# Another written order for the first block of a two-block model: which matmul stands behind which

## The chip, the cores and the metric

The kernel runs on one core of a Trainium2 chip. A core has a matmul engine (TensorE; in the profile PE, and PEld for its weight loads), VectorE (DVE), ScalarE (ACT) and GpSimd (POOL), which run beside each other and wait for each other through semaphores; SyncE (SP) issues most DMAs. The metric is the device time of one execution in microseconds (us), lower is better. The kernel before takes 1187.47 us, the median of three runs (1187.04 to 1188.63).

## The reference, cut to what matters

One sequence of 256 tokens with 1024 features goes through two blocks. Only the first is touched. It projects the normed input `h` with one wide matrix into the inputs of three branches and into the logits of three gates, and adds the gated branches:

```python
h = rms_norm(x, norm1_g[l])
proj = h @ w_in[l]
p_rwkv, p_sb, q_mem, gate_logits = jnp.split(proj, cut, axis=-1)
y_a, v_first = rwkv7_branch(p_rwkv, ...)         # recurrence over time, 8 heads
y_b = stick_breaking_branch(p_sb, ...)           # causal attention, 8 heads
y_m = memory_branch(q_mem, mem, ...)             # softmax attention on 256 memory rows, 4 heads
ys = jnp.stack([y_a, y_b, y_m], axis=2)
branch_out = jnp.einsum('btnc,ncd->btnd', ys, w_branch[l])
gates = jax.nn.sigmoid(gate_logits.reshape(b, t, N_BRANCH, D_MODEL))
x = x + jnp.sum(gates * branch_out, axis=2) @ w_out[l]
x = x + conv_ffn(x, ...)
```

The memory branch makes its keys and values from the normed memory: `kv = rms_norm(mem, mem_g) @ w_kv`, keys in the first 512 columns, values in the other 512. The second block (an mLSTM mixer, a sparse attention and two more FFNs) follows.

## The kernel before, in words

**Weights.** Every weight matrix is cut into tiles of 128 x 128, and `weight_tiles` (L59) lays them in DRAM in the order in which the program uses them, eight to a block of 512 KB. `Stream` (L220) loads a block over SP's queue into one of three buffers (`wstg`), and splits it into a rounded high part on ScalarE (`whi`, L238) and the rest on VectorE (`wlo`, L239), three buffers each. `W.take` hands out the next tiles and sees to it that blocks up to two ahead are asked for. A product with a tile is three matmuls: high by high, high by low part of the activations, low by high. `fp_tile` (L368) makes 128 output features for all 256 tokens from 8 (or 4) tiles; `tp_group` (L381) makes 512 output columns with tokens on the partitions, from 32 tiles, four at a time.

**The written order.** The first block is traced under a manual schedule for TensorE: its instructions run as the program writes them, up to `order.close()` (L1062). The other engines' order, and that of SP's DMAs, is set by a planner that simulates the program. To interleave the small matmuls of the branches with the weight products, each branch is a Python generator, a chain. `flow.tick` (L277) is called for each weight tile; at every tile whose number is a multiple of `GRID`, each chain whose time has come runs up to its next `yield n`, which asks to be called again n tiles later. A step writes its matmuls into TensorE's order at once, behind the tiles so far; `flow.join` (L285) writes all that is left of a chain in one go.

**The order before**, by number of weight tiles taken. 0 to 64: keys of the memory (32 tiles, accumulators from `ps_r`), then its values; beside them `x1_chain` (L523) makes the normed input X1, and the keys are normed and transposed (`qk_feat`, L509). 64 to 176: `rw_proj` (L886), 14 x 8 tiles for the RWKV branch, its chain `run_rwkv` (L701) beside it. 176 to 304: four `tp_group`s, queries of the memory, then queries, keys and values of the attention (L986 to L991); each is normed on ScalarE and VectorE, and transposed on TensorE 16 tiles after its chain has started. 304 to 592: three rounds of eight, one round for each branch (L999): a gate of 8 tiles into the left half of a PSUM accumulator, `Tanh` of it on ScalarE, a branch product of 4 tiles into the right half of the same accumulator, and the gated sum on VectorE. There are four such accumulators (`ps_acc`). The memory is the first round, the attention the second, the RWKV the third; before a round's first product its chain is joined.

**The RWKV chain** computes norms of the keys (`rw_norms`), prepares and scores four pairs of heads (`rw_prep`, `rw_scores`), then inverts small triangular blocks: the blocks `rw_ba` go to DRAM and come back in another layout (L742, L743), VectorE solves them in 15 steps (L746, L748), the results go to DRAM again (L751) and come back into `rw_krv` and `rw_z` by 24 small loads (L753, L756), all issued by SP. `yield 64` (L757) stands between this and the first matmul on the results (`rw_lt`, L774). Two levels of products and four steps of a scan follow, and the output norm. **The attention chain** `sticks` (L941) has per pair of heads: scores (`sb_z`), mask and softplus on VectorE and ScalarE, a cumulative sum on TensorE (`sb_c`), exponential, and the product with the values (`sb_o`). Its work buffer `sb_ze` shares one buffer (tag `sbt`) with `rw_ba`.

Of the kernel before, what the change touches and what calls it, by code (L numbers as in the profile page):

```python
# [18 lines left out]
KD = D // 128  # L19
# [7 lines left out]
STARTS = (82, 148, 181, 247, 279)  # L27
GRID = 2
HEAD = 4
# [13 lines left out]
def _tp(w):  # L43
    k, n = w.shape
    return w.reshape(k // 128, 128, n // 512, 4, 128).transpose(2, 0, 3, 1, 4).reshape(-1, 128, 128)
# [13 lines left out]
def weight_tiles(i):  # L59
    w_in = i["w_in"][0]  # L60
    rw = _fp(w_in[:, :1792]).reshape(14, KD, 128, 128)[RWKV_ORDER].reshape(-1, 128, 128)
    out = [_tp(i["w_mem_kv"][0]), rw, _tp(w_in[:, 3328:3840]), _tp(w_in[:, 1792:3328])]
    for n in (2, 1, 0):
        g = _fp(w_in[:, 3840 + n * D:3840 + (n + 1) * D]).reshape(KD, KD, 128, 128)
        b = _fp(i["w_branch"][0, n]).reshape(KD, 4, 128, 128)
        out.append(np.concatenate([g, b], axis=1).reshape(-1, 128, 128))
    out += [_fp(i["w_out"][0]), _up(i["w_up"][0], True), _fp(i["w_down"][0])]
    aw = i["a_w_in_2"][0]
    gt = np.zeros((D, 128), np.float32)
    gt[:, 0:4] = aw[:, 3072:3076]  # L70
    gt[:, 32:36] = aw[:, 3076:3080]
    out += [_fp(gt), _fp(aw[:, :1024]), _tp(aw[:, 1024:2048]), _fp(aw[:, 2048:3072]),
            _fp2(i["a_w_out_2"][0]), _up(i["f_w_up_2"][0], False), _fp(i["f_w_down_2"][0])]
    wkv = i["w_kv_2"]
    for g in range(2):
        s = slice(g * 512, (g + 1) * 512)
        out += [_tp(i["b_w_q_2"][0][:, s]), _tp(wkv[:, :D][:, s])]
    out.append(_tp(wkv[:, D:]))
    out += [_fp2(i["b_w_o_2"][0]), _up(i["f_w_up_2"][1], False), _fp(i["f_w_down_2"][1])]
    return out  # L80
# [111 lines left out]
def body(tc, a, out, voff, coff, tap=None, upto=99):  # L192
# [11 lines left out]
    def ps_acc(name="acc"):  # L204
        return psum.tile([128, 512], F32, name=name, tag="acc", bufs=4)
# [14 lines left out]
    class Stream:  # L220
        pos = 0
        hi, lo = {}, {}
# [157 lines left out]

    def tp_group(X, ps=ps_acc):  # L381

        po = [ps(), ps()]
        for k in range(KD):
            hi, lo = W.take(4)
            for tt in range(2):
                s = slice(tt * 128, (tt + 1) * 128)
                PE.matmul(po[tt], X.H[:, k, s], hi, start=(k == 0), stop=False)  # L388
                PE.matmul(po[tt], X.L[:, k, s], hi, start=False, stop=False)  # L389
                PE.matmul(po[tt], X.H[:, k, s], lo, start=False, stop=(k == KD - 1))  # L390
            flow.tick(4)
        return po
# [111 lines left out]
    def s4(name):  # L504
        return mp.tile([128, 4, T], F32, name=name, tag=s4tag[name])
# [3 lines left out]
    def qk_feat(po, st, nh, gain, name):  # L509
        rs = head_rs(po, nh, st and st.ev, name)  # L510
        dst = feat[name] = s4(name)
        qn = [normed(po, tt, rs, nh, name + "n") for tt in range(2)]
        yield 16
        for tt in range(2):
            tok_to_feat(qn[tt], dst, tt, gain)

    def v_tok(X, st, dst):
        po = tp_group(X)
        for tt in range(2):
            A.activation(dst[:, tt], po[tt], AF.Identity, scale=st.rs[:, tt:tt + 1] if st else 1.0, bias=0.0)  # L520
        return dst

    def x1_chain():  # L523
        yield 20
        sm._rows()
        yield 20
        s1._rows()
        yield 10
        s1._spread()
        for k in range(KD):  # L530
            V.scalar_tensor_tensor(x0[:, k], x0[:, k], vec("norm1_g", k), s1.bc, op0=OP.mult, op1=OP.mult)
            split(X1.H[:, k], X1.L[:, k], x0[:, k])
# [18 lines left out]
    x1c = flow.start(x1_chain())  # L551
    pmk = tp_group(XM, ps_r)
    flow.start(qk_feat(pmk, sm, 4, vec("mem_k"), "mkT"))
    mv = s4("mv").rearrange("p a t -> p (a t)").rearrange("p (a c) -> p a c", c=512)
    v_tok(XM, sm, mv)
    flow.join(x1c)
# [68 lines left out]
    def rw_prep(p, rs, SC, BK, UV, wc):  # L625
# [33 lines left out]
        for par in range(2):  # L659
# [5 lines left out]
            V.tensor_tensor(BK[s, p, :, o], ch(kp, par), ch(iw, par), op=OP.mult)  # L665
        yield 14
        PE.matmul(pb[:, T:2 * T], con("bones"), sx, start=True, stop=True)
# [33 lines left out]
    def run_rwkv():  # L701
# [10 lines left out]
        while em.i < 6:  # L712
            yield 1
        yield 8
        rs = rw_norms()
        for p in range(4):
            while em.i < 8 + 2 * p:
                yield 1
            yield 6
            yield from rw_prep(p, rs, SC, BK, UV, wc)  # L720
            yield 8
            rw_scores(p, SC, BK, BA, RB, BKT)
# [64 lines left out]
        for c in range(4):  # L787
# [8 lines left out]
            A.activation(P_[64:128], pp4[64:128, :, 1], AF.Copy)  # L796
            yield 6
            pu = ps_r("rw_puu")
# [6 lines left out]
            A.activation(UV[64:128, :, c, 1], puv[64:128], AF.Copy)  # L805
            yield 6
            if c < 3:
# [74 lines left out]
    class Emit:  # L882
        i = 0
# [31 lines left out]
    def memory(po):  # L915
        yield from qk_feat(po, None, 4, gains[:, 1:2], "mqT")
        YM = done["yM"] = Half("yM", "a")
        yield 4
        nxt = me_scores(0)
        for h in range(4):  # L920
            yield 10
            pr_ = nxt
            pt = ps_m("me_t")
            pt2 = pt.rearrange("p (m t) -> p m t", t=T)
            for mt_ in range(2):
                for tt in range(2):
                    PE.transpose(pt2[:, mt_, tt * 128:(tt + 1) * 128], pr_[:, tt, mt_ * 128:(mt_ + 1) * 128], ident)
            pT = mp.tile([128, 2, T], F32, name="me_pT", bufs=1)
            A.activation(pT, pt2, AF.Copy)
            if h < 3:  # L930
                nxt = me_scores(h + 1)
            yield 6
            po_ = ps_m("me_o")
            for mt_ in range(2):
                PE.matmul(po_[:, :T], mv[:, mt_, h * 128:(h + 1) * 128], pT[:, mt_], start=(mt_ == 0), stop=(mt_ == 1))
            split(YM.H[:, h], YM.L[:, h], po_[:, :T])
            dbg(f"ym{h}", YM.H[:, h].bitcast(F32))
        yield 4


    def sticks():  # L941
# [5 lines left out]
        for p in range(4):  # L947
# [14 lines left out]
            split(eh, el, e)  # L962
            yield 24
            for par in range(2):
# [7 lines left out]
            A.activation(z, z, AF.Exp)  # L972
            yield 12
            po_ = ps_m("sb_o")
# [8 lines left out]
            dbg(f"yb{p}", YB.H[:, p].bitcast(F32))  # L983
        yield 4

# [4 lines left out]
    sv = s4("sv").rearrange("p a t -> p (a t)").rearrange("p (a c) -> p a c", c=512)  # L990
    v_tok(X1, None, sv)  # L991
    flow.join(csk)
# [6 lines left out]
    for n, chain, Yn in ((2, cm, "yM"), (1, cb, "yB"), (0, ca, "yA")):  # L999
        for m in range(KD):  # L1000
            pg = ps_acc()
            fp_tile(pg[:, 0:T], X1)
            g = mp.tile([128, T], F32, name="gt", bufs=2)
            A.activation(g, pg[:, 0:T], AF.Tanh, scale=0.5)  # L1004
            flow.join(chain)
            fp_tile(pg[:, T:2 * T], done[Yn], 4)
# [355 lines left out]
```

## Time and profile before

| | |
|---|---|
| median of three runs | 1187.47 us |
| the profiled execution's own time | 1190.39 us |
| its span, first to last instruction | 1188.5 us |
| PE busy | 1121.6 us (94%) |
| PEld busy | 1038.9 us (87%) |
| DVE busy | 879.0 us (74%) |
| ACT busy | 668.7 us (56%) |
| end of the first block's gated sums in the trace | 383.7 us |

The page's busy shares are averages over the whole execution. "Granted clock" is the share of full speed (2.4 GHz) that TensorE's clock was given in a stretch: 1.00 is full, 0.50 is the lower of its two levels, 1.2 GHz. In square brackets a timeline shows how long the engine sat idle before an instruction, and what ended that. Times of a timeline are us from the span's start.

### The profile page before, as it was taken

What the parts mean: (1) busy time and instruction counts of PE and PEld (TensorE: products, weight loads), DVE (VectorE), ACT (ScalarE), POOL (GpSimd) and SP (SyncE); (2) the same over time, 40 slices, a digit from 0 to 9 for tenths busy, and PEclk for the clock granted to TensorE, in tenths of its full rate; (3) what the DMA queues carried; (4) which work ended last, traced back from release to release, by engine and by line L of the source; (5) the groups of instructions that cost most, each with busy time, mean ns of one, the idle gap of its engine ahead of it and who ended that gap; (6) DMA issues with size and microseconds to landing.
All of it is one profiled execution on the core that took longest, in us unless ns stands there. A gap on an engine that the chain in (4) does not pass through costs nothing.

```text
span 1188.5 us, 21261 instructions
## 1 busy us (share of the span) xinstructions
PE 1121.6 (94%) x8266; PEld 1038.9 (87%) x8266; DVE 879.0 (74%) x1671; ACT 668.7 (56%) x1141; POOL 53.3 (4%) x133
## 2 busy tenths in 40 slices
PE   8999788886888999999999999999999999999998
PEld 5897677775888999998898999999888899999987
DVE  7779664445555789996665689999778967999963
ACT  7756443444434576665454667666554665766642
POOL 2101000000000100000010010000001001000000
PEclk9989888987999999999999999999999999999999
DMA  8534322211345555656655465555665544556663
GB/s 281 172 120 130 98 69 92 90 53 54 112 155 163 196 177 183 189 180 189 190 178 172 132 195 178 180 187 184 186 194 193 160 135 150 181 180 190 180 203 116
DMA packets 60789, 189.28 MB, mean 159 GB/s; under 512 B 12688, under 2 KB 14992, under 8 KB 60688
## 3 DMA queue, kind: packets, MB, share of 16 engines
q1 hardware_dynamic: 59792, 186.51, 50.1%
q8 instruction: 65, 1.06, 0.4%
q0 software_dynamic: 320, 1.05, 0.3%
q10 hardware_dynamic: 576, 0.37, 0.1%
q14 instruction: 36, 0.29, 0.1%
HBM read 186.46 MB, written 1.44 MB: 158 GB/s over the span
## 4 chain that ended last, share of the span: by engine, by line
PE 75%; ACT 2%; DVE 2%; issue 1%; ACTq 0%
PE acc L364 16%; PE acc L365 16%; PE acc L366 16%; PE acc L1043 10%; PE acc L1045 5%; PE acc L390 2%; PE acc L388 2%; PE acc L389 2%; ACT whi L238 1%; DVE wlo L239 1%; ACT gt L1004 0%; PE tr L497 0%; PE mb_s L1286 0%; PE rw_pp L792 0%; PE mb_o L1315 0%
## 5 line engine op out<-in xcount | busy, mean ns | idle before, releaser
L238 ACT ACTIVATE whi<-wstg 128x1024 fp32r<-128x1024 f32 (+1 forms) x453 | 375.3, 851 | 350.6 <-PE acc L365 135.5
L239 DVE TENSOR_TENSOR wlo<-wstg,whi 128x1024 fp32r<-128x1024 f32 (+1 forms) x453 | 431.3, 969 | 170.7 <-ACT whi L238 162.9
L1043 PE MATMUL acc<-ffy,whi 128*128 128x512 f32 x528 | 183.2, 395 | 0.0
L1045 PE MATMUL acc<-ffy,wlo 128*128 128x256 f32 x528 | 144.5, 278 | 0.0
L1043 PEld LDWEIGHTS acc<-ffy,whi 128*128 128x128 f32 x528 | 98.0, 188 | 22.0
L1045 PEld LDWEIGHTS acc<-ffy,wlo 128*128 128x128 f32 x528 | 99.3, 188 | 1.4
L365 PE MATMUL acc<-x6l,whi 128*128 128x256 f32 x352 | 99.3, 284 | 0.8 <-DVE x6l L342 0.8
L365 PE MATMUL acc<-x2l,whi 128*128 128x256 f32 x352 | 99.2, 283 | 0.0
L364 PE MATMUL acc<-x2h,whi 128*128 128x256 f32 x352 | 99.2, 283 | 0.0
L364 PE MATMUL acc<-x4h,whi 128*128 128x256 f32 x352 | 99.0, 283 | 0.0
L364 PE MATMUL acc<-x6h,whi 128*128 128x256 f32 x352 | 98.9, 283 | 0.0
L365 PE MATMUL acc<-x4l,whi 128*128 128x256 f32 x352 | 98.9, 283 | 0.0
L366 PE MATMUL acc<-x2h,wlo 128*128 128x256 f32 x352 | 97.8, 283 | 0.0
L366 PE MATMUL acc<-x4h,wlo 128*128 128x256 f32 x352 | 97.6, 283 | 0.0
L366 PE MATMUL acc<-x6h,wlo 128*128 128x256 f32 x352 | 97.6, 283 | 0.0
L364 PE MATMUL acc<-x1h,whi 128*128 128x256 f32 x304 | 90.0, 296 | 0.0
L365 PE MATMUL acc<-x1l,whi 128*128 128x256 f32 x304 | 88.3, 290 | 1.3 <-DVE x1l L339 1.3
L366 PE MATMUL acc<-x1h,wlo 128*128 128x256 f32 x304 | 87.7, 289 | 0.0
L1087 ACT ACTIVATE ffa<-ffu,ffcv 128x256 f32<-128x256 f32 x132 | 70.7, 587 | 0.0
L365 PEld LDWEIGHTS acc<-x6l,whi 128*128 128x128 f32 x352 | 67.5, 192 | 1.2 <-DVE x6l L342 1.2
L365 PEld LDWEIGHTS acc<-x2l,whi 128*128 128x128 f32 x352 | 67.6, 192 | 0.0
L364 PEld LDWEIGHTS acc<-x2h,whi 128*128 128x128 f32 x352 | 67.6, 192 | 0.0
(597 smaller groups left out, 2684.8 us busy)
## 6 DMA issues: line engine op xcount, KB each, us to landing
wstg<-in_wst_dram SPq DMA_DIRECT2D x343, 512.0 KB, 3.6
wstg<-in_wst_dram SPq DMA_DIRECT2D x4, 256.0 KB, 5.3
mst<-in_memT_dram SPq DMA_DIRECT2D x4, 256.0 KB, 6.0
x<-in_xT_dram SPq DMA_DIRECT2D x2, 512.0 KB, 7.8
xt<-in_xT_dram POOLq DMA_DIRECT2D x4, 256.0 KB, 6.1
out_dram<-xt SPq DMA_DIRECT2D x8, 128.0 KB, 3.6
cst<-in_cst_dram SPq DMA_DIRECT2D x1, 673.0 KB, 8.3
small<-in_small_dram SPq DMA_DIRECT2D x1, 512.0 KB, 8.9
```

Source lines behind the costliest of these rows:

```text
L238: A.activation(hi[:, p], src[:, p], AF.Copy)
L239: V.tensor_tensor(lo[:, p], src[:, p], hi[:, p].bitcast(F32), op=OP.subtract)
L364: PE.matmul(o, hi, xh, start=start, stop=False, **kw)
L365: PE.matmul(o, hi, xl, start=False, stop=False, **kw)
L366: PE.matmul(o, lo, xh, start=False, stop=stop, **kw)
L388: PE.matmul(po[tt], X.H[:, k, s], hi, start=(k == 0), stop=False)
L389: PE.matmul(po[tt], X.L[:, k, s], hi, start=False, stop=False)
L390: PE.matmul(po[tt], X.H[:, k, s], lo, start=False, stop=(k == KD - 1))
L1043: PE.matmul(ps, hi, X[k].rearrange("p s t -> p (s t)"), start=(k == 0), stop=False, skip_group_check=True)
L1045: PE.matmul(ps[:, 0:T], lo, X[k][:, 0], start=False, stop=(k == kn - 1), skip_group_check=True)
L1087: A.activation(ac[:, g], u[:, g, 2:], AF.Identity, scale=cv[:, c + 2:c + 3], bias=cv[:, c + 3:c + 4])
```

## The change

It alters the order in which the first block is written, and the layout of the weights in DRAM to match. No product, and no instruction on its data, is added or removed.

- Keys and values of the memory are made together (`tp_groups`): for each 128-row slice of the memory four tiles for the keys, then four for the values, so a weight block holds one slice's eight tiles instead of two slices' four. The keys' norm starts behind the last of these products.
- The gate of output tile m+1 is written ahead of the branch product of tile m, in each round. The join of a round's chain now comes after two gates (16 tiles) instead of one.
- `GRID` is 4 instead of 2, and the yields of the chains are other numbers, most of them multiples of 4. A normed query or key is transposed 24 tiles after its chain has started (was 16), a scan step waits 8 tiles (was 6), an attention pair takes 20 + 8 + 4 tiles (was 24 + 12), a memory head 8 + 4 (was 10 + 6).

```diff
-GRID = 2
+GRID = 4
...
-    out = [_tp(i["w_mem_kv"][0]), rw, _tp(w_in[:, 3328:3840]), _tp(w_in[:, 1792:3328])]
+    kv = i["w_mem_kv"][0].reshape(KD, 128, 8, 128).transpose(0, 2, 1, 3).reshape(-1, 128, 128)
+    out = [kv, rw, _tp(w_in[:, 3328:3840]), _tp(w_in[:, 1792:3328])]
...
-        out.append(np.concatenate([g, b], axis=1).reshape(-1, 128, 128))
+        out.append(g[0])
+        for m in range(KD):
+            out += ([g[m + 1]] if m + 1 < KD else []) + [b[m]]
...
-    def tp_group(X, ps=ps_acc):
-        po = [ps(), ps()]
+    def tp_groups(X, *groups):
         for k in range(KD):
-            hi, lo = W.take(4)
-            for tt in range(2):
...
-            flow.tick(4)
+            for po in groups:
+                hi, lo = W.take(4)
+                for tt in range(2):
...
+                flow.tick(4)
+
+    def tp_group(X):
+        po = [ps_acc(), ps_acc()]
+        tp_groups(X, po)
         return po
...
         qn = [normed(po, tt, rs, nh, name + "n") for tt in range(2)]
-        yield 16
+        yield 24
...
     def x1_chain():
-        yield 20
+        yield 28
         sm._rows()
-        yield 20
+        yield 8
         s1._rows()
-        yield 10
+        yield 12
         s1._spread()
...
-    pmk = tp_group(XM, ps_r)
+    pmk, pmv = [ps_r(), ps_r()], [ps_acc(), ps_acc()]
+    tp_groups(XM, pmk, pmv)
+    mv = s4("mv").rearrange("p a t -> p (a t)").rearrange("p (a c) -> p a c", c=512)
+    v_tok(pmv, sm, mv)
     flow.start(qk_feat(pmk, sm, 4, vec("mem_k"), "mkT"))
-    mv = s4("mv").rearrange("p a t -> p (a t)").rearrange("p (a c) -> p a c", c=512)
-    v_tok(XM, sm, mv)
     flow.join(x1c)
...
-        yield 14
+        yield 16
         PE.matmul(pb[:, T:2 * T], con("bones"), sx, start=True, stop=True)
...
-        yield 8
+        yield 12
         rs = rw_norms()
         for p in range(4):
             while em.i < 8 + 2 * p:
                 yield 1
-            yield 6
+            yield 4
             yield from rw_prep(p, rs, SC, BK, UV, wc)
...
-            yield 6
+            yield 8
             pu = ps_r("rw_puu")
...
-            yield 6
+            yield 8
             if c < 3:
...
-            yield 10
+            yield 8
             pr_ = nxt
...
-            yield 6
+            yield 4
             po_ = ps_m("me_o")
...
-            yield 24
+            yield 20
             for par in range(2):
                 pc = ps_m("sb_c")
...
-            yield 12
+            yield 8
             po_ = ps_m("sb_o")
...
-        yield 4
+            yield 4
...
     for n, chain, Yn in ((2, cm, "yM"), (1, cb, "yB"), (0, ca, "yA")):
-        for m in range(KD):
+        def gate(m):
             pg = ps_acc()
             fp_tile(pg[:, 0:T], X1)
             g = mp.tile([128, T], F32, name="gt", bufs=2)
             A.activation(g, pg[:, 0:T], AF.Tanh, scale=0.5)
+            return pg, g
+
+        nxt = gate(0)
+        for m in range(KD):
+            pg, g = nxt
+            if m + 1 < KD:
+                nxt = gate(m + 1)
             flow.join(chain)
             fp_tile(pg[:, T:2 * T], done[Yn], 4)
```

## Rows read from the trace of the kernel before

**Rows 1.** The page's head and its first part: the span, then an engine's busy time, share of the span and instructions.

```profile
span 1188.5 us, 21261 instructions
PE 1121.6 (94%) x8266; PEld 1038.9 (87%) x8266; DVE 879.0 (74%) x1671; ACT 668.7 (56%) x1141; POOL 53.3 (4%) x133
```

**Rows 2.** Busy time by stage: the stretch and its length, busy us (and instructions) of PE, PEld, DVE, ACT and POOL, the granted clock, the DMA engines' share, GB/s.

```profile
0.00:37.50 37.50, 30.68 (x125) 20.69 (x125) 28.80 (x93) 26.74 (x70) 8.60 (x31) 1.00 0.75 261
37.50:71.00 33.50, 30.96 (x230) 30.29 (x229) 20.55 (x56) 19.73 (x49) 2.19 (x6) 0.90 0.45 142
71.00:116.50 45.50, 45.02 (x301) 38.01 (x299) 43.15 (x91) 30.44 (x59) 4.74 (x11) 1.00 0.47 139
116.50:134.80 18.30, 12.52 (x55) 9.89 (x53) 11.34 (x24) 6.56 (x15) 0.81 (x3) 0.81 0.18 58
134.80:176.50 41.70, 35.34 (x171) 28.67 (x170) 31.26 (x86) 19.72 (x37) 0.00 (x0) 0.92 0.34 83
176.50:292.50 116.00, 89.68 (x964) 80.50 (x963) 58.30 (x94) 50.81 (x67) 2.47 (x4) 0.86 0.24 78
292.50:383.70 91.20, 78.11 (x648) 74.25 (x647) 49.06 (x70) 35.98 (x53) 2.37 (x4) 0.99 0.42 129
...
440.00:460.00 20.00, 20.00 (x169) 20.00 (x168) 19.00 (x34) 12.62 (x21) 0.00 (x0) 1.00 0.62 190
```

**Rows 3.** Who waited for whom on TensorE from 0 to 480 us: the waiting line, what it waited for, us in total, times, the longest.

```profile
PE acc L364 <- ACT gt L1004: 28.3, 22, 4.4
PE sb_c L966 <- ACT sb_e L338: 7.0, 1, 7.0
PE tr L497 <- DVE mqTn L487: 5.7, 1, 5.7
PE tr L497 <- DVE skTn L487: 3.3, 1, 3.3
PE tr L497 <- DVE sqTn L487: 2.9, 1, 2.9
```

**Rows 4.** The chain that ended last, in order of time (start, us, what): the Tanh of two gates, with another gate between them.

```profile
356.93 0.39 ACT gt L1004
...
367.90 0.39 ACT gt L1004
```

**Rows 5.** Timeline of TensorE in the first 64 us, three of the instructions that it sat idle for.

```profile
22.08 0.50 PE L388 MATMUL acc<-whi,xmh 128*128 128x512 f32 x1 [1.36 <-ACT whi L238]
...
39.27 0.39 PE L365 MATMUL acc<-x1l,whi 128*128 128x256 f32 x1 [1.05 <-DVE x1l L339]
...
63.06 1.01 PE L619 MATMUL rw_pst<-cst,rw_sq 128*128 128x2 f32 x4 [0.89 <-ACT rw_sq L617]
```

**Rows 6.** Three stretches behind long waits of TensorE, in the columns of rows 2.

```profile
122.50:128.00 5.50, 5.43 (x19) 4.72 (x19) 0.81 (x3) 2.43 (x3) 0.00 (x0) 0.55 0.00 0
...
200.00:206.00 6.00, 6.00 (x50) 5.66 (x51) 2.13 (x4) 1.63 (x2) 0.00 (x0) 0.51 0.01 3
...
258.00:267.50 9.50, 9.50 (x45) 9.50 (x46) 1.79 (x3) 1.83 (x3) 0.00 (x0) 0.51 0.18 55
```

**Rows 7.** Timeline of TensorE: the scores of the last pair of RWKV heads, and the first matmuls on the inverse.

```profile
134.77 1.16 PE L688 MATMUL rw_ps<-rw_sc,rw_bk 64*128 64x128 f32 x16
...
176.45 2.08 PE L766 MATMUL rw_lt<-rw_krv,rw_ba 64*64 64x64 f32 x64
```

**Rows 8.** Timeline of SP's DMA issues for the inverse of the RWKV branch: start, us over the whole group, line, DMA, count.

```profile
137.58 3.77 SPq L742 DMA_DIRECT2D dn<-rw_ba  x8
...
160.48 0.33 SPq L751 DMA_DIRECT2D dz<-rw_xb  x1
...
163.49 3.82 SPq L753 DMA_DIRECT2D rw_z<-dz  x8
167.35 7.91 SPq L756 DMA_DIRECT2D rw_krv<-dz  x14
```

**Rows 9.** Timeline of VectorE: the first step of the solve, then the mask and the split of the attention's first and second pair.

```profile
145.81 0.16 DVE L746 TENSOR_TENSOR rw_tb<-rw_xb,rw_nb 128x1 f32<-128x1 f32 x1 [1.08 <-DMA rw_nb<-dn]
...
192.36 1.02 DVE L957 TENSOR_TENSOR sb_ze<-sb_z,cst 128x384 f32<-128x384 f32 x2 [0.24 <-PE rw_lt L766]
...
200.61 0.96 DVE L339 TENSOR_TENSOR sb_e<-sb_ze,sb_e 128x768 fp32r<-128x768 f32 x1 [0.87 <-ACT sb_e L338]
...
218.89 1.02 DVE L957 TENSOR_TENSOR sb_ze<-sb_z,cst 128x384 f32<-128x384 f32 x2 [0.81 <-PE sb_z L954]
...
226.73 0.96 DVE L339 TENSOR_TENSOR sb_e<-sb_ze,sb_e 128x768 fp32r<-128x768 f32 x1 [0.26 <-ACT sb_e L338]
```

**Rows 10.** Timeline of TensorE at the join of the attention chain: the last pair.

```profile
278.42 0.92 PE L954 MATMUL sb_z<-sqT,skT 64*128 64x256 f32 x6 [1.34 <-DVE yB L339]
286.36 0.69 PE L966 MATMUL sb_c<-sb_e,sb_nt 128*128 128x384 f32 x1 [7.03 <-ACT sb_e L338]
...
290.95 1.12 PE L978 MATMUL sb_o<-sb_ze,sv 128*64 128x256 f32 x4 [1.52 <-ACT sb_ze L972]
```

**Rows 11.** The feed of a weight block: the page's sixth part (issues, KB each, median us from issue to landing), then the two splits in the timelines of ScalarE and VectorE.

```profile
wstg<-in_wst_dram SPq DMA_DIRECT2D x343, 512.0 KB, 3.6
...
359.03 1.06 ACT L238 ACTIVATE whi<-wstg 128x1024 fp32r<-128x1024 f32 x1 [1.71 <-PE acc L365]
...
360.12 1.22 DVE L239 TENSOR_TENSOR wlo<-wstg,whi 128x1024 fp32r<-128x1024 f32 x1
```

More of the change, by code (lines that the diff above doesn't have):

```diff
@@ L379, in fp_pairs @@
             evac(i, m, ps.rearrange("p (j t) -> p j t", t=T))
-    def tp_group(X, ps=ps_acc):
-        po = [ps(), ps()]
+    def tp_groups(X, *groups):
         for k in range(KD):
-            hi, lo = W.take(4)
-            for tt in range(2):
[L387 to L390, printed above, removed]
-            flow.tick(4)
+            for po in groups:
+                hi, lo = W.take(4)
+                for tt in range(2):
+                    s = slice(tt * 128, (tt + 1) * 128)
+                    PE.matmul(po[tt], X.H[:, k, s], hi, start=(k == 0), stop=False)
+                    PE.matmul(po[tt], X.L[:, k, s], hi, start=False, stop=False)
+                    PE.matmul(po[tt], X.H[:, k, s], lo, start=False, stop=(k == KD - 1))
+                flow.tick(4)
+    def tp_group(X):
+        po = [ps_acc(), ps_acc()]
+        tp_groups(X, po)
         return po
@@ L512, in qk_feat, with v_tok @@
         qn = [normed(po, tt, rs, nh, name + "n") for tt in range(2)]
-        yield 16
+        yield 24
         for tt in range(2):
             tok_to_feat(qn[tt], dst, tt, gain)
-    def v_tok(X, st, dst):
-        po = tp_group(X)
+    def v_tok(po, st, dst):
         for tt in range(2):
@@ L990, in body @@
     sv = s4("sv").rearrange("p a t -> p (a t)").rearrange("p (a c) -> p a c", c=512)
-    v_tok(X1, None, sv)
+    v_tok(tp_group(X1), None, sv)
     flow.join(csk)
```

## The prediction

> **What bounds the kernel now.** I read the page first: TensorE is busy for 1121.6 us of a span of 1188.5 [rows 1]. That share is an average over unlike stages, so the second view is the table by stage. From 383.7 us on (the residual product of the first block, both FFNs and the second block, untouched by the change) TensorE has nothing left to give: a stretch such as 440 to 460 runs 169 matmuls in 20 us, busy throughout. Before that, in the first block, 383.7 us of work hold some 61 us without a matmul and stretches at a granted clock of 0.81 to 0.92 [rows 2]. The third view, who waited for whom on TensorE up to 480 us, names these: 28.3 us in 22 waits for the Tanh of a gate, 7.0 for the attention's split, 11.9 in three waits for normed queries and keys [rows 3]. The reader should see that TensorE follows the written order there: one late input stops every matmul behind it. So what is to be forecast is the sum of these waits, the half-clock stretches behind the long ones, and what becomes late in their place.
>
> From the fill stretch a weight tile (three matmuls) costs 3 x 20 / 169 = 0.355 us [rows 2]; block one takes 592 of them. I number the moments of the written order by the tiles taken before them, counted through the loops and the yields of both versions.
>
> **The gates.** The work is the same: 24 gates of 8 tiles, 24 products of 4. Now the Tanh reads the first half of an accumulator, the product writes the other half of the same one, and the product's first matmul waits until the Tanh is through: two gates take 10.97 us (356.93 to 367.90), 5.48 each, where 12 tiles need 4.26 [rows 4]. That is 1.22 us per gate, restart included. With the next gate between, the Tanh has 8 tiles of gate m+1 (2.84 us) and, from the second gate on, also the 4 of the product before: 4.26 us in steady state. The longest of the waits is 4.4 us [rows 3], so little is left of any. Of the 24 gates 15 lie after the forced join of the attention, from 292.5 to 383.7: 15 x 1.22 = 18.3 us. Two accumulators are held where one was, of four; that costs nothing while VectorE adds a product up within the next gate, and the price if it does not is its own lag, some 1 us.
>
> By the Trainium skill (Perfetto Trace Analysis, "Identifying the Most-Contended Engine") a busy matmul row is a bad measure of headroom and the weight loads' share a good one. Beside the stage from 292.5: matmuls leave 91.2 - 78.1 = 13.1 us, loads leave 17.0 [rows 2]. My 18.3 from the period is nearer the second; by the first the forecast would be 5 us later.
>
> **The first stage (to 37.5 us).** Keys and values together need one 128-row slice of the memory per weight block instead of two, and the normalisation of the keys moves behind the last product, out of the path to X1. After its warm-up TensorE waits at eight places until 40 us, 6.3 us in all (the longest, 1.36, at 22.08; the last, 1.05, at 39.27 [rows 5]). No row shows the new order. Bounds: all eight gone (6.3 us), or 1 us lost because both pairs of accumulators now end together. Most waits are for weight splits, which stay, so I take 2 us. The step of the RWKV norms comes 6 tiles later (128, was 122), but its reciprocal root has only 8 tiles before the first preparation instead of 14; TensorE waited there already (0.89 us at 63.06, [rows 5]), and the stage's granted clock of 0.90 over 33.5 us [rows 2] is another 3.4 us. I charge 1 us (between 0 and 3).
>
> **Queries of the memory.** The transposes of the normed memory queries move from tile 226 to 236. VectorE is 95% busy from 71 to 116.5 (43.15 of 45.5) [rows 2], so it will not finish sooner; TensorE does 10 tiles (3.55 us) of its 5.7 us wait [rows 3]. The wait left is 2.2 us, and the half-clock stretch behind it (122.5 to 128 at 0.55, [rows 6], worth 2.5 us) goes. Gain 6.0. The RWKV scores of the last pair then come 6.0 + 2 - 1 - 0.7 (2 tiles later in the order) = 6.3 us earlier: at 128.5 instead of 134.8 [rows 7].
>
> **The inverse's round trip to DRAM: what is late next.** In the following 41.7 us the waits for the normed queries and keys of the attention (2.9 and 3.3 us, [rows 3]) go, since 24 tiles now cover them instead of 16, and 3.3 us of lost clock (0.92 granted, [rows 2]) with them. TensorE by itself would need 41.7 - 6.2 - 3.3 + 1.6 (one more memory step falls in here) = 33.8. But the scores feed a chain that TensorE does not set: SP issues 8 small DMAs at 137.58 and, when VectorE has solved (from 145.81), the stores at 160.48; then it issues 24 small loads, the last group of 14 from 167.35 to 175.26 [rows 8, 9]. The first matmul that needs them starts at 176.45 [rows 7], less than 2 us behind the last issue. Both versions leave 64 tiles for this, so the cover was just enough and is now about 8 us short. I keep 41.7 us: that matmul comes at 128.5 + 41.7 = 170.2. Bounds: the solve's window of 14.7 us also holds splits, norms and a softmax, so at best (these gone, some 6 us by my count of its instructions) 6 us less; at worst 2 more, from weight splits that now come faster in VectorE's line. SP's weight loads queue behind the 24, but the next block (tile 320) is needed 12 tiles later, which covers landing and split.
>
> **Scans and attention beside the gates (176.5 to 292.5).** Of these 116 us, 26.3 are idle and half-clock stretches cost about 12.7 (3.0 + 1.7 + 4.7 + 3.3; [rows 2, 6], which show the first and the third), so the work is 77; six more tiles fall into the stretch now (to the join at tile 416): 79. Added is what stays or is new:
> - behind the 8 us wait at 170 a stretch at half clock, as behind a wait for a Tanh (200 to 206 at 0.51, [rows 6]): 3.0.
> - first attention pair: its scores are masked into a buffer that the RWKV still reads until its last `rw_lt`; from there (192.36) to the split's end (201.57) is 9.2 us [rows 9]. The step that needs it is now tile 328, 8 tiles and two small products (5.1 us) behind `rw_lt`, where it was 12 tiles and a gate wait: 4.1 us of new wait and 3.0 of half clock.
> - second and third pair: 20 tiles plus scan steps, 10.2 and 9.7 us, against a chain of 8.8 (218.89 to 227.69, [rows 9]): nothing.
> - the forced join: the last pair starts at 404 and is due at 416, so 5.0 us of work cover a chain of 8.8, where before the whole pair ran uncovered (waits of 1.34, 7.03 and 1.52 us, [rows 10]). Left: 3.8 + 1.5, and 2.5 of half clock.
> - short waits at gates and scan steps: 1.8.
>
> Sum 19.7, so 98.7 us instead of 116. The finer yields of the scans (8 for 6) and of the memory (8 and 4 for 10 and 6) cost nothing by themselves: each step's copies, under 2 us, stand beside at least 4 tiles; uncovered, that price would return at each of 8 scan steps. Steps at every fourth tile move a step by at most 2 tiles (0.7 us).
>
> **Rest and sum.** From the join to 383.7: 91.2 - 18.3 - 1.2 (half clock until 295) - 8 tiles fewer (2.8) = 68.9. The block ends at 170.2 + 98.7 + 68.9 = 337.8 instead of 383.7: 45.9 us earlier. The rest of the kernel is bound by TensorE and moves along. The profiled execution took 1190.39, 1.9 around its span of 1188.5 and 2.9 above the median of the three runs, 1187.47. Against its own time I get 1144.5, against the median 1141.6: I forecast **1142 us**.
>
> **Rivals.**
> - *The middle stage gives its gain back* (22%). There ScalarE and VectorE have 51 and 58 us of work [rows 2] and strict queues; if weight splits, table loads and splits of the attention delay one another whenever TensorE runs ahead, the residual doubles to 40 us: 1142 + 20 = 1162. For it: a third of the forecast already is new waits. Against: VectorE would be only 60% busy.
> - *Nothing new is late* (13%): the DRAM chain shortens with the faster TensorE and the attention keeps pace. 6 us and some 13 us come on top: 1123. Against it the load issues that end just before their user [rows 7, 8].
> - *The gates still wait* (4%): the Tanh of gate m+1 is queued on ScalarE behind something that needs product m. Then 24 x 1.22 = 29 us stay: 1171. Against it: nothing in the code between them needs that product but two adds on VectorE.
> - *Slower* (4%): the feed of weights becomes the bound of the gate stages. From tile 304 on, 36 blocks are used; the forecast wants one per 2.84 us. Landing 3.6, the split on ScalarE 1.06 and on VectorE 1.22 [rows 11] make 5.9 us for one block; three buffers hide this (440 to 460 shows it, [rows 2]). If ordering lets only one block be in flight, 36 x (5.9 - 2.84) = 110 us are lost against 45.9 won: 1252. It decides from 4.1 us per block on, where the loss reaches 45.9.
>
> **How the numbers follow.** The forecast holds 57% (own range 1130 to 1155). The range 1121 to 1165 reaches into the two neighbours and leaves about 16% outside, the last two rivals and edges. What this measurement tells from no change is about 0.2%, 2.4 us. All cases but the last are faster; I leave 2% for same: faster 0.94, same 0.02, slower 0.04.
>
> **What would show it.** Right: no wait of a product for a Tanh above 1 us in the last 15 gates and a period near 4.3 us; a wait for DMA at the first `rw_lt`, near 170 us, of 5 to 9 us; one wait of about 4 us at the first `sb_c` and another at the last; the first block's end near 338. Wrong: a period above 5 us with idle that ends on weight splits, `rw_lt` without a wait before 166, or a first block that ends after 350.

## The result and the profile after

The changed kernel takes **1157.26 us** (median of four executions, 1154.01 to 1159.61) beside 1187.33 before: ratio 0.9743, 95% interval [0.9716, 0.9769], 30 us faster. The profiled execution is the fastest of the four, 1154.01 us of its own. The page's head and first part, to set beside [rows 1]:

```profile
span 1152.2 us, 21257 instructions
PE 1107.9 (96%) x8266; PEld 1030.4 (89%) x8266; DVE 877.0 (76%) x1671; ACT 666.9 (58%) x1141; POOL 53.3 (5%) x133
```

The same matmuls in a span 36.3 us shorter. Busy time by stage, cut at the same moments and in the columns of [rows 2] (length, PE, PEld, DVE, ACT, POOL, granted clock, DMA share, GB/s):

```profile
0.00:38.30 38.30, 30.72 (x117) 21.11 (x117) 25.17 (x77) 24.35 (x66) 8.43 (x31) 0.96 0.73 256
...
116.50:130.10 13.60, 10.39 (x47) 8.40 (x45) 9.36 (x21) 5.62 (x12) 0.89 (x3) 0.87 0.23 78
130.10:176.60 46.50, 36.16 (x185) 29.72 (x185) 33.42 (x91) 21.68 (x41) 0.00 (x0) 0.91 0.38 97
176.60:270.70 94.10, 83.50 (x962) 76.40 (x962) 50.65 (x78) 49.67 (x66) 2.48 (x4) 0.92 0.29 91
270.70:344.20 73.50, 70.42 (x619) 69.19 (x618) 50.33 (x80) 33.47 (x50) 2.36 (x4) 0.98 0.47 145
...
300.00:340.00 40.00, 40.00 (x334) 39.88 (x333) 26.83 (x41) 19.68 (x29) 0.00 (x0) 1.00 0.58 177
```

The stretch from the last RWKV scores to `rw_lt` has grown (46.5 us, was 41.7), the scans have shrunk (94.1, was 116), and in the gates TensorE runs without a gap: 334 matmuls in 40 us. Who waited for whom on TensorE up to 480 us, in the columns of [rows 3]:

```profile
PE sb_c L973 <- ACT sb_e L341: 7.2, 2, 4.9
PE rw_lt L773 <- DMA rw_krv<-dz: 6.7, 2, 3.5
PE pr L391 <- ACT whi L241: 3.8, 3, 2.6
PE tr L504 <- DVE mqTn L494: 3.2, 1, 3.2
PE rw_py L871 <- DVE rw_krv L859: 3.1, 1, 3.1
PE tr L504 <- DVE skTn L494: 2.1, 1, 2.1
```

The 28.3 us for the Tanh are gone from the list. New are the waits for the inverse's loads (`rw_lt`) and for the RWKV output norm (`rw_py`). Longer is the one for a weight split of the first stage: 3.8 us at `pr`, where the kernel before had 1.0 there and 1.4 at the values' `acc`. Where they stand, in the timeline of TensorE (start, us, then the instruction; in brackets the idle time before it and what ended it):

```profile
23.55 0.50 PE L391 MATMUL pr<-whi,xmh 128*128 128x512 f32 x1 [2.63 <-ACT whi L241]
...
123.78 1.95 PE L504 MATMUL tr<-cst,mqTn 128*128 128x128 f32 x8 [3.21 <-DVE mqTn L494]
130.07 1.16 PE L695 MATMUL rw_ps<-rw_sc,rw_bk 64*128 64x128 f32 x16
172.94 0.45 PE L773 MATMUL rw_lt<-rw_krv,rw_ba 64*64 64x64 f32 x2 [3.51 <-DMA rw_krv<-dz]
176.62 3.65 PE L773 MATMUL rw_lt<-rw_krv,rw_ba 64*64 64x64 f32 x62 [3.24 <-DMA rw_krv<-dz]
200.47 0.44 PE L973 MATMUL sb_c<-sb_e,sb_nt 128*128 128x384 f32 x1 [2.28 <-ACT sb_e L341]
202.22 0.60 PE L974 MATMUL sb_c<-sb_e,sb_nt 128*128 128x384 f32 x1 [1.30 <-DVE sb_e L342]
264.66 0.69 PE L973 MATMUL sb_c<-sb_e,sb_nt 128*128 128x384 f32 x1 [4.89 <-ACT sb_e L341]
269.24 1.13 PE L985 MATMUL sb_o<-sb_ze,sv 128*64 128x256 f32 x4 [1.52 <-ACT sb_ze L979]
...
289.25 1.15 PE L871 MATMUL rw_py<-cst,rw_krv 128*64 128x64 f32 x32 [3.08 <-DVE rw_krv L859]
```

Four moments of the block, read from the timelines of four kernels, with the forecast among them. The forecast's 337.8 for the block's end stood 8 tiles of the residual product behind its first matmul, as 383.7 did before; 2.9 us are taken off to give the mark used here.

| us from the start | before | forecast | changed | gates alone (below) | last kernel (below) |
|---|---|---|---|---|---|
| scores of the last RWKV pair | 134.8 | 128.5 | 130.1 | 133.3 | 127.8 |
| `rw_lt` (where it stops again: the rest) | 176.4 | 170.2 | 176.6 | 174.9 | 172.4 |
| join: first product of yB | 292.4 | 268.9 | 270.7 | 272.2 | 251.3 |
| first residual matmul | 380.8 | 334.9 | 344.2 | 342.0 | 323.9 |

So the block ends 9.3 us later than forecast: 6.4 are lost by `rw_lt`, 4.6 won in the middle, 7.5 lost behind the join. The rest of the distance from 1142 to 1157 is the choice of execution: before, the profiled one was 2.9 us slower than the median; after, it is 3.25 us faster. Of the 45.9 us of gain that were forecast, 30 came.

### The profile page after: what moved, and what is told of

The parts are those of the page before. It is cut to its first block, busy times and chain, and to the rows that moved or that the text cites. A ratio compares the mean times of both kernels' runs of the same rounds, so it can differ in the third digit from the quotient of the medians.

```text
span 1152.2 us, 21257 instructions
## 1 busy us (share of the span) xinstructions
PE 1107.9 (96%) x8266; PEld 1030.4 (89%) x8266; DVE 877.0 (76%) x1671; ACT 666.9 (58%) x1141; POOL 53.3 (5%) x133
## 4 chain that ended last, share of the span: by engine, by line
PE 86%; DVE 6%; ACT 3%; issue 2%; DMA 1%; SPq 1%; POOL 0%; ACTq 0%; DVEq 0%; POOLq 0%
PE acc L367 18%; PE acc L368 18%; PE acc L369 18%; PE acc L1057 11%; PE acc L1059 5%; PE acc L391 3%; PE acc L392 3%; PE acc L393 3%; DVE wlo L242 2%; ACT whi L241 1%; PE tr L504 1%; DMA mst<-in_memT_dram 1%; SPq L763 1%; PE rw_lt L773 0%; PE rw_pp L799 0%
```

## The experiments

Two accounts stood against each other at first. By the first, the time up to `rw_lt` is held by the chain through DRAM, so that the gates bring nearly the whole gain and what the other edits save ahead of that point is lost there. By the second, each part brings its own share, the gates about what the forecast gave them behind the join. Later expectations name the wait or the chain that they are about. All ratios are to the kernel before, in runs of the same chip.

### The gates alone, and all but the gates

`e1_gates` is the kernel before with the edit below and the matching order of the weights (not shown); `e2_nogates` is the changed kernel with both taken back.

```diff
-        for m in range(KD):
+        def gate(m):
             pg = ps_acc()
...
+            return pg, g
+
+        nxt = gate(0)
+        for m in range(KD):
+            pg, g = nxt
+            if m + 1 < KD:
+                nxt = gate(m + 1)
```

> The kernel before with one part alone: the next gate written between a gate and its product. Theory 1 (the gates carry nearly all of the gain, since 24 x 1.22 = 29 us of waits for a Tanh vanish and all lie behind the first matmul on the inverse): 1155 to 1162 us. Theory 2 (the steps and yields carry a good half, the gates give part of theirs back at the scans): 1168 to 1175.

Measured: 1151.34 us, ratio 0.9691 [0.9676, 0.9705].

> The changed kernel with the gates written as before (everything else as changed). Theory 1: 1182 to 1188, since what the queries' later transposes win is waited for again at the first matmul on the inverse. Theory 2: 1168 to 1175.

Measured: 1174.96 us, ratio 0.9891 [0.9877, 0.9906].

The gates alone gain 37 us, more than either account allowed and 6 more than the whole change. By the table of moments 18.7 us of this lie between `rw_lt` and the join and 18.6 behind it. The expected 29 us took 1.22 for every gate; but of the 28.3 us of Tanh waits before, the seven in that middle stretch make 15.2, and its granted clock rises from 0.86 to 0.93 when they go. The other edits gain 13 by themselves and cost 6 on top of the gates. In the table they win 3.2 us up to the scores, lose 4.9 up to `rw_lt`, win 3.2 up to the join and lose 3.7 behind it: 2.2 us of cost. The rest of the 6 is mostly that the changed kernel was profiled in a fast execution. The two gains overlap, and the waits of TensorE show a part of it. Before, the Tanh waits were 28.3 us in 22 [rows 3]; with the other edits alone they are

```profile
PE acc L365 <- ACT gt L1009: 18.7, 18, 3.1
PE sb_c L971 <- ACT sb_e L339: 8.6, 2, 6.5
PE rw_lt L771 <- DMA rw_krv<-dz: 8.5, 2, 5.1
```

Of the 13 us, 9.6 were thus saved in waits that the gates' edit removes anyway. And with the gates alone, the same view has no wait at `rw_lt` and none at `rw_py`; one Tanh wait of 1.7 us is left, and old waits stay:

```profile
PE sb_c L968 <- ACT sb_e L340: 7.2, 1, 7.2
PE tr L499 <- DVE mqTn L489: 5.8, 1, 5.8
PE tr L499 <- DVE skTn L489: 3.3, 1, 3.3
PE tr L499 <- DVE sqTn L489: 2.9, 1, 2.9
```

### The other parts, each taken back

`e3_nokv` computes keys, then values, as before, in the changed kernel, with the old yields of `x1_chain`; `e4_noyield` keeps keys and values together and takes the finer steps back (the grid and the other yields of the diff but those of `x1_chain`; one of them is shown).

```diff
-        yield 28
+        yield 20
...
-    pmk, pmv = [ps_r(), ps_r()], [ps_acc(), ps_acc()]
-    tp_groups(XM, pmk, pmv)
+    pmk = tp_group(XM, ps_r)
```

> The changed kernel with keys and values of the memory one after the other again (and the old yields of the X1 chain). Theory 1: within 3 us of the changed kernel (1154 to 1160), since the first stage took as long as before. Rival: the interleaving buys or costs 4 us or more.

Measured: 1152.42 us, 0.9705 [0.9683, 0.9727]. Outside the 3 us expected: by the medians keys and values together cost about 5 us. The spreads overlap (1150.8 to 1156.9 here), but three of these four executions are faster than every one of the unaltered kernel; in the profiles the first residual matmul comes 2.0 us earlier (342.2). So the sign is shown, and the size lies at 2 to 5 us.

```diff
-GRID = 4
+GRID = 2
...
-        yield 24
+        yield 16
```

> The changed kernel with steps at every second tile and the old yields of all chains but X1's. Theory 1: 1154 to 1163; the waits for the normed queries come back (about 12 us with their half clock), but the wait for the inverse's loads goes with them, and the attention pairs get their 24 tiles back. Theory 2: 1170 or more.

Measured: 1156.79 us, 0.9731 [0.9715, 0.9747]: by the medians the finer steps are worth nothing in sum. Its waits for normed queries and keys are back (5.8, 5.6 and 2.6 us) and `rw_lt` starts at 183.4 without a wait. TensorE reaches the scores 9.0 us earlier with the fine steps (130.1 instead of 139.1). In the profiles 6.8 of these are left at `rw_lt`, and 5.1 at the first residual matmul (349.3 here); against the second profile of the unaltered kernel (348.0, below) only 1.3 are left there.

### The chain through DRAM

`e5_solve_cut` leaves out steps 8 to 15 of the triangular solve on VectorE, so its time is that of a chain cut short.

```diff
-        for t in range(1, 16):
+        for t in range(1, 8):
```

> The changed kernel without steps 8 to 15 of the 15-step solve on VectorE (so the inverse is that of the first 8 rows of each block only). Theory 1 (the first products on the inverse wait for a chain through VectorE and SP, and nothing behind it is as late): 7 us of wait and some 3 us of half clock go: 1146 to 1150. Rival (what is not waited for there is waited for at the next late input, the attention's split or the output norm): 1155 or more.

Measured: 1144.72 us, 0.9631 [0.9609, 0.9653]. The store of the inverse goes out at 148.4 instead of 160.1, `rw_lt` has no wait, and these 11.7 us arrive at the end in full (12.5 by the medians). The solve was on the path. TensorE by itself needs 36.5 us from the scores to `rw_lt` here (129.3 to 165.8), where the prediction counted 33.8. Why the solve takes longer in the changed kernel than before is in VectorE's groups over the solve (instruction, count, then busy us and mean ns of one, then idle); before, from 145.8 to 160.5:

```profile
L746 DVE TENSOR_TENSOR rw_tb<-rw_xb,rw_nb 128x1 f32<-128x1 f32 (+14 forms) x15 | 4.6, 304 | 1.4 <-DMA rw_nb<-dn 1.1
L748 DVE TENSOR_REDUCE rw_xb<-rw_tb 128x1 f32<-128x1 f32 (+14 forms) x15 | 3.6, 238 | 0.3
L239 DVE TENSOR_TENSOR wlo<-wstg,whi 128x1024 fp32r<-128x1024 f32 x2 | 2.4, 1224 | 0.9 <-PE me_o L935 0.9
```

and after, from 140.5 to 160.1:

```profile
L242 DVE TENSOR_TENSOR wlo<-wstg,whi 128x1024 fp32r<-128x1024 f32 x5 | 6.1, 1221 | 0.1
L753 DVE TENSOR_TENSOR rw_tb<-rw_xb,rw_nb 128x1 f32<-128x1 f32 (+14 forms) x15 | 4.5, 302 | 1.0 <-DMA rw_nb<-dn 0.8
L755 DVE TENSOR_REDUCE rw_xb<-rw_tb 128x1 f32<-128x1 f32 (+14 forms) x15 | 3.5, 236 | 0.2
```

The solve's own steps cost the same. Five weight splits stand among them instead of two (3.7 us more), with softmax steps and the normed keys' squares. It is the finer steps that bring them: `e4_noyield`, which has the new gates and the old steps, has two splits again and takes 14.8 us from the first step to the last copy, where the changed kernel takes 19.6.

```profile
L242 DVE TENSOR_TENSOR wlo<-wstg,whi 128x1024 fp32r<-128x1024 f32 x2 | 2.5, 1226 | 1.1 <-ACT whi L241 1.1
```

That TensorE, no longer stopped for the queries and keys, calls for the next block sooner is the likely reason; no run tried it by itself. In the changed kernel the first step starts 5.3 us earlier than before, the last ends 0.3 earlier.

`e6_z_on_pool` moves 8 of SP's 24 loads of the inverse to GpSimd.

```diff
-            nc.sync.dma_start(Z[r, :, j], dz[1, b].rearrange("u i j -> i u j"))
+            nc.gpsimd.dma_start(Z[r, :, j], dz[1, b].rearrange("u i j -> i u j"))
```

> The changed kernel with 8 of the 24 small loads behind the solve issued by GpSimd instead of SP. Theory 1: SP's line is 8 x 0.49 = 3.9 us shorter, the wait at the first product on the inverse shrinks by as much: 1152 to 1155. Rival (the loads' landing, not SP's issue, sets the time, or GpSimd issues more slowly than SP): within 1.5 us of the changed kernel.

Measured: 1153.18 us, 0.9705 [0.9686, 0.9725], 4 us less than the change by the medians; the spreads overlap, with three of the four executions faster than every one of the unaltered kernel. In the timelines of the issues, SP has its loads out in 8.70 us where it needed 4.84 + 7.02, and GpSimd issues the rest beside it:

```profile
161.49 8.70 SPq L763 DMA_DIRECT2D rw_krv<-dz  x16
...
162.06 4.72 POOL L760 DMA_DIRECT2D rw_z<-dz  x8 [41.27 <-DMA dz<-rw_xc]
```

The Trainium skill (Trainium Kernel Development and Optimization, "Key Constraints") says that issuing DMAs from several engines only saves the sequencer's issue time, since all run on the same DMA engines. The trace agrees: the loads are small, issue time is what was late, and one wait of 3.0 us at `rw_lt` is left of 6.7.

### The first attention pair's buffer, and the sums of the memory rows

`e7_own_buffer` gives the masked scores `sb_ze` memory that the RWKV does not hold.

```diff
-            ze = mp.tile([128, 4, 384], F32, name="sb_ze", tag="sbt")
+            ze = xpool.tile([128, 2048], F32, name="sb_ze", tag="x8b", bufs=1)...
```

> The changed kernel with the attention's work buffer in a slot of its own, not that of the RWKV blocks. Theory: the mask of the first pair no longer waits for the last product on those blocks, so the wait at the first cumulative sum (2.28 + 1.30 us) and about 2 us of half clock behind it go: 1151 to 1154. Rival: the wait moves to the second pair or to the join: within 1.5 us.

Measured: 1149.44 us, 0.9673 [0.9656, 0.9689], somewhat better than expected. The first pair's wait is gone, that at the join stays, and in return a product of the inverse's first level (`rw_lz`) is late:

```profile
PE rw_lt L773 <- DMA rw_krv<-dz: 6.6, 2, 3.4
PE sb_c L973 <- ACT sb_e L341: 4.9, 1, 4.9
...
PE rw_lz L773 <- DVE rw_krv L788: 2.6, 1, 2.6
```

The `rw_py` wait fell from 3.1 to 0.4 us as well; why it did was not tried by itself.

`e8_rows_early` puts the sums of the memory rows at tile 20 instead of 32.

```diff
-        yield 28
+        yield 16
         sm._rows()
-        yield 8
+        yield 20
```

> The changed kernel with the sums of the memory's squares written at tile 20 instead of 32 (the other two steps of that chain stay at 40 and 52). Theory 3 (the 5 us that the joint keys and values cost come from this one step: its matmul frees the only buffer of the sums, for which the squares of x, and behind them on ScalarE the weight splits, wait): 1151 to 1154. Rival (the interleaving itself costs it, by more accumulators or a later X1): within 1.5 us of the changed kernel.

Measured: 1154.25 us, 0.9713 [0.9689, 0.9737]; 3 us less than the change with overlapping spreads, so as a time it is inconclusive. The place is shown: X1's products start at 33.1 instead of 38.3. In the changed kernel, the timelines of VectorE and ScalarE have

```profile
20.96 0.69 DVE L442 TENSOR_TENSOR st_acc<-st_sq 128x512 f32<-128x512 f32 x1 [2.89 <-PE st_ps L462]
```

```profile
21.74 1.15 ACT L437 ACTIVATE st_sq<-x 128x512 f32<-128x512 f32 x2 [3.46 <-DVE sm_v L464]
22.79 3.77 ACT L241 ACTIVATE whi<-wstg 128x256 fp32r<-128x256 f32 x12
```

One buffer holds the running sum of squares. It comes free when TensorE has summed the memory rows, a step that the change moved from tile 22 to 32. Until then the squares of `x` wait on ScalarE, twelve weight splits wait behind them in its queue, and TensorE waits 2.63 us for the first of these. But the 5 us won here are 2.1 at `rw_lt` (170.8 instead of 172.9): the chain through DRAM takes the rest, and in these profiles nothing is left at the first residual matmul (344.7 for 344.2).

### The unaltered kernel once more

> The changed kernel once more, unaltered, for its spread (5.6 us over four executions, where the kernel before has 1.6) and a second trace. Theory 4 (the waits are the same from execution to execution, and what differs is how long the clock stays at its lower level behind them): median 1155 to 1159, the listed waits within 0.5 us each of those of the first trace, the half-clock time different by 1 us or more if the two executions differ by 2. Rival (the DMA round trip to DRAM differs): the waits at the first product on the inverse differ by as much as the times.

Measured: 1157.80 us, 0.9737 [0.9723, 0.9752]. The profiled execution is 3.8 us slower than the first one (1157.83). Its largest waits are the same within 0.5 us (`sb_c` 7.2, `rw_lt` 6.2, `rw_py` 3.1); the granted clock behind them is not. It is 0.81 and 0.65 from 198 to 207, 1.00 and 0.79 from 64 to 72. Two more stretches in the columns of [rows 2], first profile:

```profile
288.00:297.00 9.00, 7.75 (x102) 7.27 (x103) 5.65 (x8) 3.62 (x6) 0.00 (x0) 1.00 0.20 60
262.00:275.00 13.00, 8.52 (x49) 6.94 (x50) 4.65 (x8) 4.18 (x7) 0.00 (x0) 0.61 0.14 42
```

and second:

```profile
288.00:297.00 9.00, 6.54 (x52) 6.06 (x53) 4.51 (x11) 1.97 (x4) 0.00 (x0) 0.62 0.23 71
262.00:275.00 13.00, 7.60 (x40) 6.13 (x42) 4.67 (x8) 4.58 (x6) 0.00 (x0) 0.64 0.18 57
```

In 288 to 297, behind the `rw_py` wait, the second execution loses 9 x (1 - 0.62) = 3.4 us of clock where the first loses none. The stage from the join to the first residual matmul holds 3.0 of the 3.8 us (271.5 to 348.0, where the first has 270.7 to 344.2). The 32 products behind the wait show the clock; this line of the second execution stands beside the one of 289.25 above, where they took 1.15 us:

```profile
290.46 1.97 PE L871 MATMUL rw_py<-cst,rw_krv 128*64 128x64 f32 x32 [3.09 <-DVE rw_krv L859]
```

So about half of the 5.6 us over which the change's executions spread can come from this one wait; what makes the rest is not shown. The executions of `e1_gates`, without this wait, lie within 0.5.

### Repairs together

`e10_own_short_pairs` has the buffer of `e7_own_buffer` and shortens each attention pair by 4 tiles, so that the last pair starts earlier before its join.

```diff
             dbg(f"yb{p}", YB.H[:, p].bitcast(F32))
-            yield 4
+        yield 4
```

> The attention's own buffer, and 28 tiles for a pair instead of 32 (the last yield of a pair only after the fourth), so that the last pair's cumulative sum is due before the join. Theory: the waits at the join (4.89 + 0.30 + 1.52 us) shrink to about 1.5, and the half clock behind them (about 5 us) goes, against some 1 us at the next pair's scores: 1139 to 1143 (the own buffer alone: 1149.4). Rival: the last pair is late anyway, since its chain on ScalarE and VectorE is behind: 1146 or more.

Measured: 1147.49 us, 0.9659 [0.9645, 0.9672]: missed, only 2 us below `e7_own_buffer`. The rival named such a time, but not for what happened: the last pair is no longer late, and the waits at its cumulative sum are gone. But three `sb_z` steps now wait 2.7 us together, `rw_lt` 8.0 instead of 6.6, and the 3.1 us at `rw_py` are back.

`e11_all_repairs` joins `e6_z_on_pool`, `e8_rows_early` and `e10_own_short_pairs` and puts 8 more tiles in front of `rw_py`.

```diff
         YA = done["yA"] = Half("yA", "b")
-        yield 24
+        yield 32
```

> The changed kernel with all repairs: own buffer, 28 tiles for a pair, the memory's sums at tile 20, 8 loads on GpSimd, 32 instead of 24 tiles behind the RWKV output norm. Adding the single gains (7.8 + 8 + 3.0 + 4.1, and 3 for the norm) gives 1131; as the early gains are partly waited for again at the inverse, 1131 to 1139.

Measured: 1141.88 us, 0.9609 [0.9596, 0.9622]: better than all above and still short of what was expected, again for waits that came in place of others. `rw_py` still waits 2.2 us with its 8 tiles more. In the timeline of TensorE:

```profile
167.62 3.28 PE L773 MATMUL rw_lt<-rw_krv,rw_ba 64*64 64x64 f32 x62 [2.62 <-DMA rw_krv<-dz]
...
181.73 1.97 PE L773 MATMUL rw_lz<-rw_z,rw_tm 64*64 64x64 f32 x32 [4.73 <-DVE rw_krv L788]
```

`e12_all_and_72` gives the DRAM chain 72 tiles of cover instead of 64.

```diff
-        yield 64
+        yield 72
```

> As the one before, and 72 instead of 64 tiles between the inverse's start and the first product on it. If VectorE's solve and the loads still end last there, 1 to 4 us less than the one before; if nothing is late there any more, or the scans are late then, the same or up to 2 us more.

Measured: **1133.19 us**, 0.9532 [0.9519, 0.9545], 24 us below the change and the best of all. The 8 tiles bring 8.7 us, not 1 to 4. The same places:

```profile
172.43 2.08 PE L773 MATMUL rw_lt<-rw_krv,rw_ba 64*64 64x64 f32 x64
...
180.27 1.15 PE L773 MATMUL rw_lz<-rw_z,rw_tm 64*64 64x64 f32 x32 [0.37 <-DVE rw_krv L788]
```

`rw_lt` starts 4.8 us later than the rest did in `e11_all_repairs`, with no wait; the `rw_lz` behind it starts 1.5 us earlier, though 8 more tiles (2.8 us) stand ahead of it, and needs no restart at half clock, where `e11_all_repairs` has 0.66 granted from 181.7 to 190 (2.8 us). These three make 7.1 of the 8.0 us by which the first residual matmul comes earlier.

## Why the prediction was right and where it was wrong

**The gates: right.** No product waits for a Tanh for more than 1 us. From the last row of the stage table after, 12 tiles (36 matmuls) take 36 x 40 / 334 = 4.31 us, where 4.26 was forecast. The sum behind the join was a little too large. The groups of TensorE behind the join show 184 tiles before (120 + 32 + 32 by line) and 176 with the gates alone; without the 2.8 us of those 8 tiles, that stage gains 88.4 - 69.8 - 2.8 = 15.8 us, against 18.3 for the gates and 1.2 for the clock. Of the 3.7 us between them 2.0 are the clock: the restart behind the join stayed, with a granted clock of 0.73 over the first 7.3 us there. By the Trainium skill (Perfetto Trace Analysis, "Identifying the Most-Contended Engine") the weight loads' share is a better measure of headroom than matmul busy time. It left 17.0 us, matmuls 13.1; the 15.8 lies between, nearer the loads.

**The first stage: wrong in sign.** The step "so I take 2 us" for keys and values together counted weight splits as unmoved and forgot that the sums of the memory rows move with them and free a buffer. X1 starts at 38.3 instead of 37.5, and `e3_nokv` puts the cost of the part at 2 to 5 us.

**Queries of the memory: right, small miss.** 3.2 us of wait for 2.2 forecast; the half-clock stretch did not go altogether. The scores come at 130.1 for 128.5.

**The inverse's round trip: the mechanism right, the size wrong.** A DMA wait at the first `rw_lt` was forecast at 5 to 9 us and came with 6.7. But the step "I keep 41.7 us" failed: the chain takes 46.5. The text named weight splits "that now come faster in VectorE's line" as the bound of 2 us on that side; they are three more splits, 3.7 us, and other work came with them, with the finer steps (`e4_noyield` has neither). `e5_solve_cut` shows that the solve was on the path (11.7 us less of it, 12.5 us at the end), `e12_all_and_72` that with 8 tiles more of cover nothing waits at `rw_lt`.

**The middle: the waits right, the sum too large.** 94.1 us for 98.7. The waits at the first `sb_c` (2.28 + 1.30, forecast 4.1) and at the join (4.89 and 1.52, forecast 3.8 and 1.5) came as worked out, and some of the 2.5 us of half clock booked for the join falls behind it: 270.7 to 278 runs at 0.77.

```profile
270.70:278.00 7.30, 7.30 (x60) 6.98 (x59) 3.98 (x7) 2.21 (x4) 0.00 (x0) 0.77 0.01 2
```

Of the 4.6 us too much, 2.6 are no gain: 1.7 of that half clock and 0.9 of the last scan step only moved behind the join. The rest is not taken apart. The rival that this stage gives its gain back (1162) lies near the measured time but is not what happened: the loss stood before and behind that stage.

**Behind the join: a wait not foreseen.** 3.7 of the 7.5 us lost there are lost with the gates alone too (above). The other 3.7, against `e1_gates`, are the 3.1 us at `rw_py` and 16 products of the last scan step that moved behind the join (0.9 us). No step of the prediction looked at the RWKV output norm. Its cover is lost in two ways at once. With the gates alone the last scan step stands far ahead of the join (272.2), so that the norm runs beside the join's waits; the finer steps put it behind the join (270.7). The gates alone:

```profile
248.91 0.68 PE L837 MATMUL rw_pp<-rw_uv,rw_rb 64*64 64x64 f32 x16
```

and the changed kernel:

```profile
273.59 0.87 PE L842 MATMUL rw_pp<-rw_uv,rw_rb 64*64 64x64 f32 x16
```

There the norm's 24 tiles are all the cover it has. With the stops for a Tanh among them, in `e2_nogates` (its last scan step is behind the join too), 0.4 us of wait are left; without them 3.1.

**Number and range.** The errors of the stages (6.4 late, 4.6 early, 7.5 late) partly offset each other, which is luck and not foresight. The time lies 2 us above the likeliest case's own range and inside the wide one. Of the 15 us from 1142 the terms above make 9.3; the other 6.2 (2.9 + 3.25) are that the profiled execution before was a slow one of its kernel and that after a fast one, which a sum made against one profile cannot know.

## What to carry to other kernels

A stall on the bound engine is also cover for every chain beside it: when it is removed, go through each chain that ended just in time and give it more tiles, counting that the other engines' queues may hold more of the bound engine's feed, as VectorE's did in the solve. Gains of reorderings do not add (37 and 13 us alone, 30 together), so run each part alone before keeping it. When a step is moved, look at which buffers it frees, not only at what it needs.

## What the runs showed of the hardware

One and the same wait can cost half clock behind it or none. In seven profiles TensorE waits 3.08 or 3.09 us at `rw_py`. In four of them (the changed kernel, `e3_nokv`, `e5_solve_cut`, `e8_rows_early`) the 32 products behind the wait take 1.15 us and the next 32 start 5.0 us after them; in the other three (`e9_again`, `e6_z_on_pool`, `e10_own_short_pairs`) they take 1.97 or 1.98 us and the next start 7.7 us after them. That is 2.7 us for the same wait. What decides it, the profiles do not show. It does not make every kernel with long waits spread: `e1_gates` has waits of 7.2, 5.8 and 3.3 us, and its executions lie within 0.5 us.
